# Three converted hi/lo weight buffers in place of two in a two-layer decoder trunk

## The chip, the cores and the metric

One NeuronCore of a Trainium2 chip runs the whole program. The metric is the device time of one execution in microseconds (us). The engines are PE (TensorE, with PEld for its weight loads), DVE (VectorE), ACT (ScalarE), POOL (GpSimd) and SP (SyncE, which here issues the plain DMAs). Each engine works through its own instructions in order and waits on semaphores of the others.

## The reference

272 tokens (16 meta tokens and 256) of width 1024 go through two layers. In each layer a recurrent group and an attention group mix the tokens; then a PEER stage picks, for each token and each of 8 heads, 16 of 16384 one-neuron experts:

```python
for l in range(DEPTH):
    z = rms_norm(h, mix_norm_g[l]) @ w_in[l]
    y_lru = rg_lru(...) * gelu(gate)
    y_att = mla_group(...)
    h = h + concat(rms_norm(y_lru), rms_norm(y_att)) @ w_out[l]
    h = h + peer(rms_norm(h, ffn_norm_g[l]), wq, subkeys, u, v)
# peer: s = (h @ wq) . subkeys; top 16 of the 16 x 16 sums; gates = softmax
uc = take(u, experts);  act = gelu(einsum('cd,ckd->ck', h, uc))
vc = take(v, experts);  out = einsum('ck,ckd->cd', gates * act, vc)
```

## The kernel before

All large weights come as blocks of 128 x 1024 fp32 (0.524 MB), in one list `order`: per layer 14 blocks of w_in, 8 of w_out, 16 of wq, 128 of uT and 128 of v. The mixing uses w_in and w_out; PEER uses the rest. For most tokens PEER is computed densely: all 16384 neurons (uT, then gelu, times a gate that is zero where an expert was not picked, then v). The gates are built for eight tokens at a time by one-hot tiles (`oha`, `ohb`: L950 to L957), PE products into a PSUM bank `ps_g` (L966), and a multiplication into `act` (`mult`, L976, with ACT's copy in L978 for the part not yet computed). For the last 32 tokens of layer 0 and 48 of layer 1 PEER is sparse: 16 experts of one head and token fill a partition each, and a gather (L1067, an indirect DMA issued by POOL) brings 128 rows of u or v into a tile. DVE consumes it: `dot` (L1050) multiplies rows of u with the tokens, `acc` (L1054) adds rows of v. There are 96 gathers of each layer, spread between the blocks of uT and v: some of u and v in uT, the others in v, one per about two blocks.

Both kinds of tile, blocks and gathers, take turns in one pool `raw` of PF = 7 buffers. `issue` starts the load of an entry of `order` as soon as the entry seven places ahead of it is converted. `conv` takes a block from `raw` and splits it into two fp16 halves: hi on ACT (L216), lo = block - hi on DVE (L217). They lie in a pool `hl`, so that PE can compute hi x (hi, lo) and lo x hi: 16 and 8 matmuls a block (`mm3`, L242 to L246, for wq and uT; `mv`, L1142, for v). A block's raw buffer is free when its lo is done, a gather's when its dot or acc is done. For v the activations themselves are split too: `ww`, by ACT L1129 and DVE L1130, for a pair of blocks at a time.

`block(kind, l, b)` returns the next pair of halves; before it does, it converts ahead:

```python
assert order[k] == (kind, l, b), (order[k], kind, l, b)
st["k"] = k + 1
conv(ahead(k, 1) + 1)
return hls.pop(k)
```

`ahead(k, n)` is the place of the n-th block after k. Converting a gather's entry means emitting its dot or acc there. The program is written in this order, but a scheduler in the language's runtime sets each engine's own order from a priority: hi and lo have a raised one (PRI = 40 places), all other work has its place in the source. Top-k, the gates and the onehot tiles (`pump`) run between the blocks on DVE and ACT.

`rows_of(g)` prepares a group of 16 sparse tokens: ACT copies L1017, PE transposes, ACT copies L1022.

Of the kernel before, what the change touches and what calls it, by code (L numbers as in the profile page):

```python
# [1 line left out]

# [1 line left out]

# [4 lines left out]
F32 = mybir.dt.float32  # L9
F32R = mybir.dt.float32r  # L10
F16 = mybir.dt.float16
# [10 lines left out]
S = 256  # L22
# [25 lines left out]
NU = (2, 2)  # L48
UB = (((64, 127, 16), (116, 124, 1)), ((60, 127, 32),))
PF = 7  # L50
ATT = ((3, 7), (1, 7))
LRU_AT = (1, 2, 3, 4)
LRU_FIRST = 0
# [88 lines left out]
def trunk(tc, a, out, dbg=None):  # L142
# [15 lines left out]
    with ExitStack() as ctx:  # L158
        per = ctx.enter_context(tc.tile_pool(name="per", bufs=1))
        raw_p = ctx.enter_context(tc.tile_pool(name="raw", bufs=PF))  # L160
        hl_p = ctx.enter_context(tc.tile_pool(name="hl", bufs=2))
        psp = ctx.enter_context(tc.tile_pool(name="psp", bufs=2, space=PSUM))
        PB = {"u": 2, "g": 2, "v": 4}

# [55 lines left out]
        def ahead(k, n):  # L220
            while n:
                k += 1
                if k < len(order) and order[k][0] != "gather":
                    n -= 1
                elif k >= len(order):
                    break
            return k

        def block(kind, l, b):
            k = st["k"]  # L230
            while order[k][0] == "gather":
                k += 1
            assert order[k] == (kind, l, b), (order[k], kind, l, b)
            st["k"] = k + 1
            conv(ahead(k, 1) + 1)
            return hls.pop(k)

        def mm3(o, w, xhi, xlo, first=True, n=8, off=0):
# [75 lines left out]
        def mixing(l, col, hh, hl, sq):  # L314
            SQ_H = [(one, sq[:, c]) for c in range(8)]
            C0 = NM if l else 0
            with tc.tile_pool(name="mix", bufs=1) as mp:
                def mt(shape, dt, name, bufs=1, tag=None):
                    return mp.tile(shape, dt, name=name, tag=tag or name, bufs=bufs)
# [323 lines left out]
                        yield from w_out_half(b, 0)  # L643

                late = []
                if l == 0:
                    s4 = [ps("v") for _ in range(4)]
                    for h in range(8):
                        w = s4[h % 4][:16, h // 4 * 16:h // 4 * 16 + 16]
                        P.matmul(w, qx[:, h, 0:16], kx[:, h, 0:16], start=True, stop=False, skip_group_check=True)  # L650
                        P.matmul(w, idb[:, 0:16], trib[:, 0:16], start=False, stop=True, skip_group_check=True)
                    mx = mt([16, 8], F32, "mx0")
                    sm = mt([16, 8], F32, "sm0")
                    p0 = mt([16, 8, 16], F32, "p0")
                    sv = mt([16, 8, 16], F32, "sv")
                    for h in range(4):
                        V.tensor_copy(sv.rearrange("p (a b) k -> p b a k", b=4)[:, h], s4[h][:16, :32].rearrange("p (a k) -> p a k", a=2))
                    V.tensor_reduce(out=mx, in_=sv, axis=AX.X, op=ALU.max)
                    V.tensor_tensor(out=p0, in0=sv, in1=bc(mx, 2, 16), op=ALU.subtract)
                    V.tensor_tensor(out=p0, in0=p0, in1=bc(rq[:16, 0, 2], 2, 16), op=ALU.mult)  # L660
                    A.activation(p0, p0, AF.Exp)
                    V.tensor_reduce(out=sm, in_=p0, axis=AX.X, op=ALU.add)
                    V.reciprocal(sm, sm)
                    tp = ps("g")
                    P.transpose(tp[:, 0:16], p0.rearrange("p a b -> p (a b)"), ident[:16, :16])
                    pt = mt([128, 256], F32, "pt", 2)
                    V.tensor_copy(pt[:, :16], tp[:, :16])
                    O = ps("u")
                    P.matmul(O[:16], pt[:, :16], v[:, 0], start=True, stop=True)
                    late.append(att_out(16, O, sm, 2, 0))  # L670

                fl = fills()
                for k, (q0, q1) in enumerate(QT):
# [22 lines left out]
                    def pv_t(h):  # L696
                        nt = k + 1
                        tp = ps("g")
                        for i in range(nt):
                            P.transpose(tp[:, i * 128:i * 128 + 128], Pm[:, h, 16 + i * 128:144 + i * 128], ident)  # L700
                        pt = mt([128, 256], F32, "pt", 2)
                        V.tensor_copy(pt[:, :nt * 128], tp[:, :nt * 128])
                        pts[h] = pt

# [20 lines left out]
                    pv_t(7)  # L725
                    pv_m(6)
                    pv_m(7)
                    pmc = mt([128, 8, 16], F32, "pmc", 2)
                    V.tensor_copy(pmc, Pm[:, :, 0:16])
                    tp = ps("g")  # L730
                    P.transpose(tp[:, 0:128], pmc.rearrange("p a b -> p (a b)"), ident)
                    pt = mt([128, 256], F32, "pt", 2)
                    V.tensor_copy(pt[:, :128], tp[:, :128])
                    P.matmul(O, pt[:, :128], v[:, 0], start=False, stop=True, skip_group_check=True)
                    V.reciprocal(sm, sm)
# [83 lines left out]
        def peer(l, col, hh, hl, rs, wq0):  # L819
            with tc.tile_pool(name="peer", bufs=1) as pp:  # L820
                SD = S - NSP[l]
                NF = NK * S - 256
                flata = pp.tile([128, NF], F32, name="act")
                act = flata[:, 0:NK * SD].rearrange("p (j t) -> p j t", t=SD)
                ready = set()
# [24 lines left out]
                ei = [egs[:, g, 0].bitcast(I32) for g in range(NG)]  # L850
                eg = [egs[:, g, 1] for g in range(NG)]
                dots = al([NG, 16], F32)
                cur[0], cur_end[0] = PS - 12800, PS
                rbs = al([T], F32)
                sk = al([2, 128], F32)
                dma(sk, a["sk"][l])
                rb = ps("g")
                rows(rs, rb, C0)
# [22 lines left out]
                i2T = pp.tile([128, S, 2], F16, name="i2T")  # L881
                gh = pp.tile([128, S, 2], F16, name="gh")
                gl = pp.tile([128, S], F32, name="gl")
                comb = pp.tile([128, 2, 128], F32, name="comb")

                bgq = []
                credit = [0.0]
# [118 lines left out]
                    yield 0.2  # L1006

                def sparse():
                    tail = [flata[:, NK * SD + i * D:NK * SD + i * D + D] for i in range(3)]
                    stage = tail[2]  # L1010
                    hrs = [tail[0], tail[1], None, None]
                    fin = []

                    def rows_of(g):
                        hr = hrs[g % 2 if g < NU[l] else 2 + g % 2]
                        for c in range(8):
                            A.activation(stage[:, c * 128:c * 128 + 128].rearrange("p (h t) -> p h t", h=8), bc(hns[:, c, g * 16:g * 16 + 16], 1, 8), AF.Copy)  # L1017
                        for c in range(0, 8, 4):
                            tp = ps("g")
                            for k in range(4):  # L1020
                                P.transpose(tp[:, k * 128:k * 128 + 128], stage[:, (c + k) * 128:(c + k) * 128 + 128], ident)
                            A.activation(hr[:, c * 128:c * 128 + 512], tp, AF.Copy)  # L1022
                        return hr

# [97 lines left out]
                    pump(PUMP[1] - prog["t"] / 960.0)  # L1122
                drain()
                pv = [ps("v") for _ in range(4)]
                ww = area("hn", F16, [128, 2, 2, 2, SD], "ww")

                def wsplit(j):
                    b = j // 2 % 2
                    A.activation(ww[:, b, 0], act[:, j:j + 2], AF.Copy)  # L1129
                    V.tensor_tensor(out=ww[:, b, 1], in0=act[:, j:j + 2], in1=ww[:, b, 0], op=ALU.subtract)  # L1130

                wsplit(0)
                for j in range(NK):
                    hi, lo = block("v", l, j)
                    if j % 2 and j + 1 < NK:
                        wsplit(j + 1)
                    wh, wl = ww[:, j // 2 % 2, 0, j % 2], ww[:, j // 2 % 2, 1, j % 2]

                    def mv(c, k):
                        o = pv[c // 2][:, (c % 2) * SD:(c % 2) * SD + SD]  # L1140
# [67 lines left out]
```

## Time and profile before

| | |
|---|---|
| median of 3 runs | 1668.75 us (1660.89 to 1672.01) |
| profiled execution | 1668.44 us, span 1666.7 us, mean clock 0.993 |
| PE / DVE / ACT / POOL busy | 1588.0 / 1503.8 / 1098.2 / 320.6 us |
| layer 0: mixing, wq and uT, v (by the first and last instructions of each) | about 0 to 140, to 538, to 846 |
| layer 1: the same | to 973, to 1364, to 1662 |

The time that an engine is busy is a mean over stages with different limits. In a row of waits the engine on the left stood still, and the instruction on the right is the one that came last; the numbers are the sum of us, how many times, and the longest one. In the view by stretch, the columns after the two times are busy us of PE, PEld, DVE, ACT and POOL, each with its number of instructions, then the granted clock of PE, the mean busy share of the DMA engines and the GB/s. PEld (loading weights) and PE (the matmuls) overlap, so their waits can be the same gap seen twice.

### The profile page before, as it was taken

Reading aid. Unit: us, or ns where it says so; the run is one execution under the profiler, and the core shown is the slowest. Engines: PE = TensorE matmul, PEld = TensorE weight load, DVE = VectorE, ACT = ScalarE, POOL = GpSimd, SP = SyncE. Lnnn points to the kernel's source line nnn. Section 1 sums busy time; section 2 is a strip of 40 time slices with the busy share of each in tenths; the row PEclk is TensorE's granted clock in tenths of the full one; section 3 lists DMA queues with packets and bytes.
Section 4 is the critical chain, followed back from the end, with each engine's and each line's share of the span. In section 5 each row is a group of like instructions: output and inputs, shape, how many; then the busy total and the mean of one; then the engine's idle time right before and its main releaser. Section 6 shows DMA issues by size and latency. Waiting matters only on the chain.

```text
span 1666.7 us, 40245 instructions
## 1 busy us (share of the span) xinstructions
PE 1588.0 (95%) x15926; PEld 1467.8 (88%) x15926; DVE 1503.8 (90%) x3074; ACT 1098.2 (66%) x2001; POOL 320.6 (19%) x256
## 2 busy tenths in 40 slices
PE   9989999999999999999999899899999999999997
PEld 6667798899999999999967687789988899999997
DVE  6889989889999999988978899997999998989886
ACT  6857565789987555555557565678988755555653
POOL 1000000101102333333210000002124124353253
PEclk9999999999999999999999999999999999999999
DMA  7305465667777999999973054567787899999995
GB/s 291 114 11 169 141 208 198 216 204 235 246 257 254 339 374 360 367 358 352 359 260 119 3 178 140 201 217 237 229 278 272 279 351 333 346 353 353 365 338 203
DMA packets 117709, 421.21 MB, mean 253 GB/s; under 512 B 14416, under 2 KB 15824, under 8 KB 117008
## 3 DMA queue, kind: packets, MB, share of 16 engines
q1 hardware_dynamic: 88592, 317.88, 54.2%
q0 software_dynamic: 28928, 100.76, 17.4%
q8 instruction: 124, 2.03, 0.5%
q14 instruction: 65, 0.53, 0.1%
HBM read 417.46 MB, written 1.05 MB: 251 GB/s over the span
## 4 chain that ended last, share of the span: by engine, by line
PE 40%; DVE 14%; DMA 5%; ACT 3%; issue 3%; POOL 1%; DVEq 0%; POOLq 0%; ACTq 0%
PE ps_v L1142 26%; DVE lo L217 6%; PE ps_u L246 3%; DMA raw<-v,act 3%; PE ps_u L242 3%; PE ps_u L243 3%; ACT hi L216 1%; PE ps_g L966 1%; DMA raw<-v 1%; POOL raw L1067 1%; DVE act L767 1%; DVE act L764 1%; PE ps_v L243 1%; PE ps_v L242 1%; PE ps_v L246 1%
## 5 line engine op out<-in xcount | busy, mean ns | idle before, releaser
L216 ACT ACTIVATE hi<-raw 128x1024 f16<-128x1024 f32 x588 | 619.8, 1055 | 430.8 <-PE ps_v L1142 208.6
L217 DVE SCALAR_TENSOR_TENSOR lo<-raw,hi 128x1024 f16<-128x1024 f32 x588 | 710.6, 1218 | 71.2 <-ACT hi L216 64.0
L1142 PE MATMUL ps_v<-ww,hi 128*128 128x224 f16 (+1 forms) x4096 | 426.8, 257 | 11.0 <-DVE ww L1130 10.1
L242 PE MATMUL ps_u<-hn,hi 128*128 128x224 f16 (+2 forms) x2112 | 413.1, 257 | 8.2 <-ACT hi L216 6.8
L243 PE MATMUL ps_u<-hn,hi 128*128 128x224 f16 (+2 forms) x2112 | 413.0, 256 | 0.0
L1142 PEld LDWEIGHTS <-hi 128*128 128x128 f16 x4096 | 382.5, 98 | 13.6 <-issue 12.5
L246 PEld LDWEIGHTS <-lo 128*128 128x128 f16 x2656 | 244.1, 98 | 54.0 <-DVE lo L217 43.2
L242 PEld LDWEIGHTS <-hi 128*128 128x128 f16 x2656 | 260.0, 98 | 27.5 <-ACT hi L216 11.5
L243 PEld LDWEIGHTS <-hi 128*128 128x128 f16 x2656 | 259.9, 98 | 14.8 <-issue 4.5
L246 PE MATMUL ps_u<-hn,lo 128*128 128x224 f16 (+2 forms) x2112 | 242.0, 257 | 25.4 <-DVE lo L217 24.7
L1142 PE MATMUL ps_v<-ww,lo 128*128 128x224 f16 (+1 forms) x2048 | 235.7, 257 | 5.4 <-DVE lo L217 5.0
L1067 POOL DMA_INDIRECT raw<-ur,act x96 | 131.2, 1367 | 467.6 <-DVE lo L217 237.4
L1067 POOL DMA_INDIRECT raw<-v,act x96 | 157.8, 1644 | 248.1 <-DVE lo L217 186.4
L1142 PEld LDWEIGHTS <-lo 128*128 128x128 f16 x2048 | 190.5, 98 | 10.8 <-DVE lo L217 10.0
L957 ACT ACTIVATE ohb<-oha,gl 128x128 f16<-128x128 f16 x432 | 138.7, 396 | 13.2 <-DVE oha L952 13.2
L1054 DVE SCALAR_TENSOR_TENSOR acc<-raw,act,acc 128x1024 f32<-128x1024 f32 x90 | 115.1, 1279 | 28.9 <-DMA raw<-v,act 28.8
L922 POOL DMA_DIRECT2D act<-comb x40 | 20.4, 518 | 599.0 <-DVE oha L952 310.6
L243 PE MATMUL ps_v<-hgx,hi 128*128 128x272 f16 (+1 forms) x480 | 113.6, 277 | 0.4 <-DVE hgx L311 0.4
L242 PE MATMUL ps_v<-hgx,hi 128*128 128x272 f16 (+1 forms) x480 | 113.3, 277 | 0.4 <-DVE hT L1183 0.3
L1050 DVE SCALAR_TENSOR_TENSOR raw<-raw,act 128x1024 f32<-128x1024 f32 x64 | 77.6, 1216 | 5.6 <-DMA raw<-ur,act 4.6
L1130 DVE TENSOR_TENSOR ww<-act,ww 128x448 f16<-128x448 f32 (+1 forms) x128 | 76.8, 600 | 0.0
L1129 ACT ACTIVATE ww<-act 128x448 f16<-128x448 f32 (+1 forms) x128 | 69.8, 547 | 0.0
(304 smaller groups left out, 1611.1 us busy)
## 6 DMA issues: line engine op xcount, KB each, us to landing
raw<-uT SPq DMA_DIRECT2D x256, 512.0 KB, 4.3
raw<-v SPq DMA_DIRECT2D x256, 512.0 KB, 6.2
raw<-wq SPq DMA_DIRECT2D x32, 512.0 KB, 3.3
raw<-w_in SPq DMA_DIRECT2D x28, 512.0 KB, 6.8
raw<-w_out SPq DMA_DIRECT2D x16, 512.0 KB, 3.3
uq<-uq SPq DMA_DIRECT2D x2, 1152.0 KB, 10.1
ukv<-ukv SPq DMA_DIRECT2D x2, 1024.0 KB, 8.2
raw<-ur,act POOLq DMA_INDIRECT x96, 6.5
```

The source lines that it names most:

```text
L216: A.activation(hi, r, AF.Copy, scale=WS)
L217: V.scalar_tensor_tensor(out=lo, in0=r, scalar=WS, in1=hi, op0=ALU.mult, op1=ALU.subtract)
L242: P.matmul(o, hi[:, s], xhi[:, c], start=first and c == 0, stop=False, skip_group_check=True)
L243: P.matmul(o, hi[:, s], xlo[:, c], start=False, stop=False, skip_group_check=True)
L246: P.matmul(o, lo[:, s], xhi[:, c], start=False, stop=c == n - 1, skip_group_check=True)
L957: A.activation(ob[:, 1, t], oe[:, t], AF.Copy, scale=gl[:, b * 8 + t:b * 8 + t + 1])
L1050: keep = V.scalar_tensor_tensor(out=t, in0=t, scalar=1.0, in1=hr, op0=ALU.mult, op1=ALU.mult, accum_out=dot[:, s:s + 1])
L1054: keep = V.scalar_tensor_tensor(out=acc, in0=t, scalar=dot[:, s:s + 1], in1=acc, op0=ALU.mult, op1=ALU.add)
L1067: G.indirect_dma_start(out=t, out_offset=None, in_=tab, in_offset=bass.IndirectOffsetOnAxis(ap=ei[g][:, s:s + 1], axis=0))
L1129: A.activation(ww[:, b, 0], act[:, j:j + 2], AF.Copy)
L1130: V.tensor_tensor(out=ww[:, b, 1], in0=act[:, j:j + 2], in1=ww[:, b, 0], op=ALU.subtract)
L1142: P.matmul(o, (hi, hi, lo)[k][:, s], (wh, wl, wh)[k], start=j == 0 and k == 0 and c % 2 == 0, stop=j == NK - 1 and k == 2, skip_group_chec ...
```

## The change

There are three hi/lo pairs instead of two (`NHL = 3`), and `block` converts two blocks ahead instead of one. The ww pairs go from two to four, and `wsplit` runs two pairs ahead. The space comes from three places: the staging area of `rows_of` is 512 columns wide instead of 1024, and is filled, transposed and copied twice; the mixing tiles `pt` and `pmc` are slices of one tile `pta` in the buffer of `sel0`, which is dead then; `comb` lies in the scratch part of the flat `act` tile. Line numbers rise by 2 to 5 (hi L216 to L218, lo L217 to L219, dot L1050 to L1054, acc L1054 to L1058, mult L976 to L980, ww L1130 to L1134). The number of instructions of each engine is the same.

```diff
 PF = 7
+NHL = 3
...
-        hl_p = ctx.enter_context(tc.tile_pool(name="hl", bufs=2))
+        hl_p = ctx.enter_context(tc.tile_pool(name="hl", bufs=NHL))
...
-            conv(ahead(k, 1) + 1)
+            conv(ahead(k, NHL - 1) + 1)
             return hls.pop(k)
...
+                pts_ = itertools.cycle((pta[:, 0:256], pta[:, 256:512]))
                 if l == 0:
...
+                    pt = next(pts_)
                     V.tensor_copy(pt[:, :16], tp[:, :16])
...
+                    pmc = pta[:, 512 + k * 128:640 + k * 128].rearrange("p (a b) -> p a b", a=8)
                     V.tensor_copy(pmc, Pm[:, :, 0:16])
...
+                NF = NK * S - 768
                 flata = pp.tile([128, NF], F32, name="act")
...
+                cur[0], cur_end[0] = PS - 13056, PS
                 rbs = al([T], F32)
                 sk = al([2, 128], F32)
+                comb = al([2, 128], F32)
                 dma(sk, a["sk"][l])
...
 
...
-                    stage = tail[2]
+                    tail = [flata[:, NK * SD + i * D:NK * SD + i * D + D] for i in range(2)]
+                    stage = flata[:, NK * SD + 2 * D:NK * SD + 2 * D + 512]
                     hrs = [tail[0], tail[1], None, None]
                     fin = []
 
                     def rows_of(g):
                         hr = hrs[g % 2 if g < NU[l] else 2 + g % 2]
-                        for c in range(8):
-                            A.activation(stage[:, c * 128:c * 128 + 128].rearrange("p (h t) -> p h t", h=8), bc(hns[:, c, g * 16:g * 16 + 16], 1, 8), AF.Copy)
                         for c in range(0, 8, 4):
                             tp = ps("g")
                             for k in range(4):
-                                P.transpose(tp[:, k * 128:k * 128 + 128], stage[:, (c + k) * 128:(c + k) * 128 + 128], ident)
+                                A.activation(stage[:, k * 128:k * 128 + 128].rearrange("p (h t) -> p h t", h=8), bc(hns[:, c + k, g * 16:g * 16 + 16], 1, 8), AF.Copy)
+                            for k in range(4):
+                                P.transpose(tp[:, k * 128:k * 128 + 128], stage[:, k * 128:k * 128 + 128], ident)
                             A.activation(hr[:, c * 128:c * 128 + 512], tp, AF.Copy)
                         return hr
...
-                ww = area("hn", F16, [128, 2, 2, 2, SD], "ww")
+                ww = area("hn", F16, [128, 4, 2, 2, SD], "ww")
 
                 def wsplit(j):
-                    b = j // 2 % 2
+                    b = j // 2 % 4
                     A.activation(ww[:, b, 0], act[:, j:j + 2], AF.Copy)
                     V.tensor_tensor(out=ww[:, b, 1], in0=act[:, j:j + 2], in1=ww[:, b, 0], op=ALU.subtract)
 
                 wsplit(0)
+                wsplit(2)
                 for j in range(NK):
                     hi, lo = block("v", l, j)
-                    if j % 2 and j + 1 < NK:
-                        wsplit(j + 1)
-                    wh, wl = ww[:, j // 2 % 2, 0, j % 2], ww[:, j // 2 % 2, 1, j % 2]
+                    if j % 2 and j + 3 < NK:
+                        wsplit(j + 3)
+                    wh, wl = ww[:, j // 2 % 4, 0, j % 2], ww[:, j // 2 % 4, 1, j % 2]
 
                     def mv(c, k):
                         o = pv[c // 2][:, (c % 2) * SD:(c % 2) * SD + SD]
```

What stands where in the order of the engines (x of the tile names are running numbers; `lo<-raw` converts a block, `acc2<-raw` and `raw,act<-raw,act` consume a gather, ww and act as above). First, DVE in v of layer 1, before: blocks 19839, 19904 and so on, gathers 19934, 19999. The tile numbers follow the order in which the tiles are loaded.

```order
L217 SCALAR_TENSOR_TENSOR lo_19972<-raw_19839,hi_19971 128x1024
L1054 SCALAR_TENSOR_TENSOR acc2_19603<-raw_19869,act_13729,acc2_19603 128x1024
L1130 TENSOR_TENSOR ww_19703<-act_13729,ww_19703 128x416
L217 SCALAR_TENSOR_TENSOR lo_20005<-raw_19872,hi_20004 128x1024
L217 SCALAR_TENSOR_TENSOR lo_20037<-raw_19904,hi_20036 128x1024
L1054 SCALAR_TENSOR_TENSOR acc2_19603<-raw_19934,act_13729,acc2_19603 128x1024
L1130 TENSOR_TENSOR ww_19703<-act_13729,ww_19703 128x416
L217 SCALAR_TENSOR_TENSOR lo_20070<-raw_19937,hi_20069 128x1024
L217 SCALAR_TENSOR_TENSOR lo_20102<-raw_19969,hi_20101 128x1024
L1054 SCALAR_TENSOR_TENSOR acc2_19603<-raw_19999,act_13729,acc2_19603 128x1024
```

After, DVE at the same place: blocks 19809, 19839, 19874, 19904, gathers 19936, 20001.

```order
L219 SCALAR_TENSOR_TENSOR lo_19942<-raw_19809,hi_19941 128x1024
L1134 TENSOR_TENSOR ww_19671<-act_13695,ww_19671 128x416
L1058 SCALAR_TENSOR_TENSOR acc2_19537<-raw_19936,act_13695,acc2_19537 128x1024
L219 SCALAR_TENSOR_TENSOR lo_19972<-raw_19839,hi_19971 128x1024
L219 SCALAR_TENSOR_TENSOR lo_20007<-raw_19874,hi_20006 128x1024
L1134 TENSOR_TENSOR ww_19671<-act_13695,ww_19671 128x416
L1058 SCALAR_TENSOR_TENSOR acc2_19537<-raw_20001,act_13695,acc2_19537 128x1024
L219 SCALAR_TENSOR_TENSOR lo_20037<-raw_19904,hi_20036 128x1024
L219 SCALAR_TENSOR_TENSOR lo_20072<-raw_19939,hi_20071 128x1024
```

Before, the gather of raw_19999 is issued when the lo of raw_19839 is done, and four lo's, two acc's and two ww's follow that lo ahead of its acc. After, the gather of raw_20001 is issued when the lo of raw_19809 is done; between it and its acc stand ww, acc, two lo's and ww. The acc moved ahead of the lo's of the blocks 19904 to 19969, which are loaded before it.

Second, DVE in v of layer 0: before,

```order
L217 SCALAR_TENSOR_TENSOR lo_8275<-raw_8169,hi_8274 128x1024
L1130 TENSOR_TENSOR ww_7870<-act_1814,ww_7870 128x448
L1050 SCALAR_TENSOR_TENSOR raw_8204,act_1814<-raw_8204,act_1814 128x1024
L217 SCALAR_TENSOR_TENSOR lo_8305<-raw_8172,hi_8304 128x1024
L217 SCALAR_TENSOR_TENSOR lo_8340<-raw_8234,hi_8339 128x1024
L1130 TENSOR_TENSOR ww_7870<-act_1814,ww_7870 128x448
L1050 SCALAR_TENSOR_TENSOR raw_8269,act_1814<-raw_8269,act_1814 128x1024
L217 SCALAR_TENSOR_TENSOR lo_8370<-raw_8237,hi_8369 128x1024
L217 SCALAR_TENSOR_TENSOR lo_8405<-raw_8272,hi_8404 128x1024
L1050 SCALAR_TENSOR_TENSOR raw_8302,act_1814<-raw_8302,act_1814 128x1024
```

and after, where the gather raw_8259 is issued when the lo of raw_8126, the first row, is done:

```order
L219 SCALAR_TENSOR_TENSOR lo_8230<-raw_8126,hi_8229 128x1024
L219 SCALAR_TENSOR_TENSOR lo_8262<-raw_8129,hi_8261 128x1024
L1054 SCALAR_TENSOR_TENSOR raw_8159,act_1800<-raw_8159,act_1800 128x1024
L1134 TENSOR_TENSOR ww_7858<-act_1800,ww_7858 128x448
L219 SCALAR_TENSOR_TENSOR lo_8295<-raw_8191,hi_8294 128x1024
L1054 SCALAR_TENSOR_TENSOR raw_8259,act_1800<-raw_8259,act_1800 128x1024
```

Before, the gather of raw_8302, issued when the lo of raw_8169 is done, has four lo's, two dots and two ww's ahead of its dot; after, the gather of raw_8259 has two lo's, a dot and a ww.

Third, DVE in uT of layer 1, at the products of the gates (`mult`, L976 and L980, two halves of 94 blocks). Before:

```order
L217 SCALAR_TENSOR_TENSOR lo_18387<-raw_18184,hi_18386 128x1024
L1120 TENSOR_TENSOR act_13729<-act_13729,gt2_14403 128x2x152
L954 TENSOR_TENSOR ohb_16085<-oha_16084,gh_13738 128x1024
L976 SCALAR_TENSOR_TENSOR act_13729<-act_13729,ps_g_18359 128x94x4
L976 SCALAR_TENSOR_TENSOR act_13729<-act_13729,ps_g_18368 128x94x4
L1050 SCALAR_TENSOR_TENSOR raw_18181,act_13729<-raw_18181,act_13729 128x1024
L217 SCALAR_TENSOR_TENSOR lo_18419<-raw_18216,hi_18418 128x1024
```

After:

```order
L219 SCALAR_TENSOR_TENSOR lo_18352<-raw_18149,hi_18351 128x1024
L1124 TENSOR_TENSOR act_13695<-act_13695,gt2_14368 128x2x152
L958 TENSOR_TENSOR ohb_16050<-oha_16049,gh_13704 128x1024
L980 SCALAR_TENSOR_TENSOR act_13695<-act_13695,ps_g_18327 128x94x4
L219 SCALAR_TENSOR_TENSOR lo_18387<-raw_18186,hi_18386 128x1024
L980 SCALAR_TENSOR_TENSOR act_13695<-act_13695,ps_g_18336 128x94x4
```

The block of raw_18184 before is that of raw_18149 after, and the next one, raw_18216, is raw_18186. Before, the lo of that next block stands behind both halves of `mult`; after, it stands between them. In uT each lo stands one block earlier against the other work on DVE.

## Rows read from the trace of the kernel before

**Rows 1.** The page, part 1: busy us, share of the span, instructions.

```profile
PE 1588.0 (95%) x15926; PEld 1467.8 (88%) x15926; DVE 1503.8 (90%) x3074; ACT 1098.2 (66%) x2001; POOL 320.6 (19%) x256
```

**Rows 2.** Busy time by stretch: PE, PEld, DVE, ACT, POOL; clock, DMA share, GB/s.

```profile
200.00:320.00 120.00, 109.51 (x1091) 102.01 (x1089) 114.69 (x368) 78.47 (x104) 2.54 (x5) 1.00 0.59 198
...
400.00:538.00 138.00, 137.22 (x1548) 136.34 (x1546) 134.91 (x197) 113.55 (x281) 20.81 (x15) 1.00 0.77 253
538.00:846.00 308.00, 303.30 (x3121) 299.74 (x3120) 278.77 (x325) 165.45 (x196) 97.40 (x85) 0.99 0.96 357
...
1020.00:1120.00 100.00, 86.76 (x900) 79.04 (x899) 99.92 (x346) 62.50 (x75) 0.00 (x0) 1.00 0.58 195
...
1200.00:1320.00 120.00, 110.64 (x1305) 105.83 (x1304) 119.99 (x183) 97.69 (x249) 31.73 (x20) 1.00 0.82 276
1320.00:1364.00 44.00, 41.74 (x463) 40.35 (x462) 41.53 (x56) 27.14 (x44) 12.40 (x10) 1.00 0.94 336
1364.00:1662.00 298.00, 285.77 (x3120) 280.61 (x3119) 257.70 (x283) 161.99 (x192) 120.52 (x61) 0.99 0.91 329
680.00:700.00 20.00, 20.00 (x211) 20.00 (x209) 18.57 (x19) 11.83 (x14) 6.47 (x6) 1.00 1.00 381
```

**Rows 3.** Waits in 195 to 538: us in total, times, longest.

```profile
ACT hi L216 <- PE ps_u L243: 41.0, 44, 1.8
...
PEld L246 <- DVE lo L217: 15.4, 26, 1.9
...
PEld L242 <- ACT hi L216: 3.7, 7, 1.1
```

**Rows 4.** Waits in 1027 to 1364.

```profile
PEld L246 <- DVE lo L217: 25.8, 40, 1.7
...
PEld L242 <- ACT hi L216: 7.5, 10, 1.6
ACT act L978 <- DVE act L976: 7.1, 8, 2.9
```

**Rows 5.** Waits in 1364 to 1662.

```profile
DVE acc L1054 <- DMA raw<-v,act: 21.5, 11, 4.1
...
PE ps_v L1142 <- DVE ww L1130: 9.6, 6, 2.6
```

**Rows 6.** Timeline of 1619 to 1629: start, duration, engine, line, operation.

```profile
1617.87 2.35 DVE L217 SCALAR_TENSOR_TENSOR lo<-raw,hi 128x1024 f16<-128x1024 f32 x2
...
1620.14 1.28 DVE L1054 SCALAR_TENSOR_TENSOR acc<-raw,act,acc 128x1024 f32<-128x1024 f32 x1
1620.49 4.52 POOL L1067 DMA_INDIRECT raw<-v,act  x1 [5.92 <-DVE lo L217]
...
1621.34 0.58 DVE L1130 TENSOR_TENSOR ww<-act,ww 128x416 f16<-128x416 f32 x1
...
1624.06 1.44 PEld L1142 LDWEIGHTS <-hi 128*128 128x128 f16 x16
...
1626.20 1.44 PEld L1142 LDWEIGHTS <-hi 128*128 128x128 f16 x16
```

**Rows 7.** Timeline of 1630 to 1636; in brackets the idle time before.

```profile
1632.21 1.28 DVE L1054 SCALAR_TENSOR_TENSOR acc<-raw,act,acc 128x1024 f32<-128x1024 f32 x1 [4.05 <-DMA raw<-v,act]
...
1634.05 0.88 PE L1142 MATMUL ps_v<-ww,hi 128*128 128x208 f16 x8 [2.60 <-DVE ww L1130]
```

**Rows 8.** The gathers of L1067, 340 to 538: from issue to landing.

```profile
DMA to landing us min/median/max: 4.2/5.0/7.8
```

**Rows 9.** The same, 538 to 846.

```profile
DMA to landing us min/median/max: 5.0/7.2/9.7
```

**Rows 10.** The same, 1164 to 1364.

```profile
DMA to landing us min/median/max: 4.0/5.3/9.7
```

**Rows 11.** The same, 1364 to 1662.

```profile
DMA to landing us min/median/max: 4.8/8.0/11.6
```

More of the change, by code (lines that the diff above doesn't have):

```diff
@@ L1 @@
 from contextlib import ExitStack
+import itertools
 import numpy as np
@@ L645, in mixing @@
                 late = []
+                pta = mt([128, 768], F32, "pta", tag="sel0")
+                pts_ = itertools.cycle((pta[:, 0:256], pta[:, 256:512]))
                 if l == 0:
@@ L665, in mixing @@
                     P.transpose(tp[:, 0:16], p0.rearrange("p a b -> p (a b)"), ident[:16, :16])
-                    pt = mt([128, 256], F32, "pt", 2)
+                    pt = next(pts_)
                     V.tensor_copy(pt[:, :16], tp[:, :16])
@@ L700, in pv_t @@
                             P.transpose(tp[:, i * 128:i * 128 + 128], Pm[:, h, 16 + i * 128:144 + i * 128], ident)
-                        pt = mt([128, 256], F32, "pt", 2)
+                        pt = next(pts_)
                         V.tensor_copy(pt[:, :nt * 128], tp[:, :nt * 128])
@@ L727, in mixing @@
                     pv_m(7)
-                    pmc = mt([128, 8, 16], F32, "pmc", 2)
+                    pmc = pta[:, 512 + k * 128:640 + k * 128].rearrange("p (a b) -> p a b", a=8)
                     V.tensor_copy(pmc, Pm[:, :, 0:16])
@@ L731, in mixing @@
                     P.transpose(tp[:, 0:128], pmc.rearrange("p a b -> p (a b)"), ident)
-                    pt = mt([128, 256], F32, "pt", 2)
+                    pt = next(pts_)
                     V.tensor_copy(pt[:, :128], tp[:, :128])
@@ L821, in peer @@
                 SD = S - NSP[l]
-                NF = NK * S - 256
+                NF = NK * S - 768
                 flata = pp.tile([128, NF], F32, name="act")
@@ L852, in peer @@
                 dots = al([NG, 16], F32)
-                cur[0], cur_end[0] = PS - 12800, PS
+                cur[0], cur_end[0] = PS - 13056, PS
                 rbs = al([T], F32)
                 sk = al([2, 128], F32)
+                comb = al([2, 128], F32)
                 dma(sk, a["sk"][l])
@@ L883, in peer @@
                 gl = pp.tile([128, S], F32, name="gl")
-                comb = pp.tile([128, 2, 128], F32, name="comb")
                 bgq = []
@@ L1008, in sparse @@
                 def sparse():
-                    tail = [flata[:, NK * SD + i * D:NK * SD + i * D + D] for i in range(3)]
-                    stage = tail[2]
+                    tail = [flata[:, NK * SD + i * D:NK * SD + i * D + D] for i in range(2)]
+                    stage = flata[:, NK * SD + 2 * D:NK * SD + 2 * D + 512]
                     hrs = [tail[0], tail[1], None, None]
```

## The prediction

> **What bounds the kernel now.** The profiled execution took 1668.44 us (span 1666.7), 0.3 us under the median of 1668.75, so I add up against the span and add that 0.3 at the end. I read the page's busy times first. TensorE is busy 1588.0 us, 95% [rows 1], but that is an average over stages, so the second view is the busy time by stretch [rows 2]: the last three columns there are the granted clock, the DMA share and GB/s. In 538 to 846 (v of layer 0) and 1364 to 1662 (v of layer 1) PE is busy 303.30 of 308 and 285.77 of 298 us: it idles 4.7 and 12.2 us. In 400 to 538, 1020 to 1120 and 1200 to 1320 VectorE (DVE) is busy 134.91 of 138, 99.92 of 100 and 119.99 of 120 us: there DVE sets the pace and PE has the gaps.
>
> The third view is the waits, by stretch. In wq and uT, PE's weight loads wait for lo 15.4 us (26 times) and for hi 3.7 us in layer 0 [rows 3], 25.8 and 7.5 us in layer 1 [rows 4]. In v of layer 1 the sequence is different [rows 5]: DVE's acc, which adds a gathered row, waits 21.5 us in 11 times for its gather's DMA, up to 4.1 us; ww stands behind acc on DVE; and PE waits 9.6 us for ww. One of these [rows 7]: acc starts at 1632.21 after 4.05 us on its DMA, and PE's matmuls at 1634.05 after 2.60 us on ww.
>
> **What the change does, part by part.** No instruction is added or removed that costs time; the order and the buffers change. A third hi/lo pair lets hi and lo run two blocks ahead of PE.
>
> (a) *wq and uT.* The stalls there sum to 52.4 us [rows 3, 4], but most lie where DVE never rests. A deeper buffer takes no work off DVE; it lets PE enter a busy stretch with one more block in hand, once. One block of v in layer 1 takes 1626.20 − 1624.06 = 2.14 us [rows 6], with 208 columns; layer 0 has 224, so 2.14 × 224 / 208 = 2.30 us. There are four such stretches, 200 to 320 and 400 to 538, 1020 to 1120 and 1200 to 1320: 2 × 2.30 + 2 × 2.14 = 8.9 us saved. In 1320 to 1364, PE idles 2.3 us with DVE at 41.53 of 44; I take half, 1.2. Against it stand the gathers of uT in layer 0: by the new order, four have only one lo and six or seven small operations between the lo that frees their buffer and their own consumer. DVE's mean instruction in 400 to 538 is 134.91 / 197 = 0.685 us [rows 2], so that is 1.2 + 6.5 × 0.685 = 5.6 us against a median landing of 5.0 and a longest of 7.8 [rows 8]: between 0 and 4 × 2.2 us; I take 1, near the median. Sum: −9.1 us, between −52 (all stalls gone) and 0.
>
> Here a rule of the Trainium skill (Perfetto Trace Analysis, Optimization Strategy) speaks the other way: gaps that repeat on the engine that should be saturated can mean that there are too few buffers. PE's repeating waits for lo would be such gaps, and by it up to 52.4 us would come back. The same page (Identifying the Most-Contended Engine) counts VectorE's occupancy as a fair measure of its limit, and DVE at 99.92 of 100 us agrees with that, so I keep 9.1.
>
> (b) *Staging.* `rows_of` now copies four blocks, transposes, copies the result, and repeats, so ScalarE (ACT) waits for PE inside it: two halves × six calls = 12 waits. The nearest row is hi's wait for PE, 41.0 us in 44 times, 0.93 each [rows 3]: 11 us if nothing hides it. ACT is busy 113.55 of 138 and 97.69 of 120 us there, and hi runs two blocks (4.6 us) ahead, which hides it. I take +1.
>
> (c) *v of layer 0.* PE idles 4.7 us, so −4.7 is the end below. The cost is that DVE's acc and dot come sooner after their buffer's release. Take T as the time from a gather's issue to its landing. DVE's durations [rows 6] are 1.17 for a lo (2.35 for two), 1.28 for acc (and for dot about the same) and 0.58 for ww; POOL issues 0.27 us after the releasing lo ends (1620.49 against 1617.87 + 2.35). Before, the least that stood between the release and the consumer was three lo's, two accs and two ww's: 3.5 + 2.6 + 1.2 − 0.3 = 7.0 us against a median T of 7.2 [rows 9]. After, by the order, seven gathers have about two lo's, one dot, one ww (3.9 us; the second excerpt of the order shows one), ten have two more accs or dots in place of one (5.2 us) and eight have 6.5. At T = 7.2 DVE would wait 7 × 3.3 + 10 × 2.0 + 8 × 0.7 = 49 us. DVE idles 308 − 278.77 = 29.2 us there, which swallows the first part: +20 is the upper end. At T = 6 it is 23 us, less than the idle time, but not in the right places. I take +4.
>
> A second rule would limit the gain here: the Trainium skill (DMA: Bandwidth & Descriptors, Where 436 GB/s comes from) puts about 358 GB/s as HBM's limit for one core. By it v of layer 0, at 357 GB/s over the whole stretch, could gain nothing. The trace moved 381 GB/s in 680 to 700 [rows 2], so the measurement leaves a few per cent.
>
> (d) *v of layer 1* decides. Here the order shows a steady pattern of two lo's, ww, acc per two blocks. Before, a gather's buffer was released by a lo after which two accs, two ww's and four lo's stood ahead of its own acc: 2.6 + 1.2 + 4.7 − 0.3 = 8.2 us at DVE's pace, about the median landing of 8.0 [rows 11]. After, 50 of the 64 gathers have only two lo's, two ww's and one acc (or dot) between (the first excerpt). Let A(n) be the start of the n-th acc. The releasing lo ends one acc and two lo's after A(n−1): 1.28 + 2.35 = 3.63 us; + 0.27 for POOL, + T, and A(n+1) can start. So two periods take at least 3.9 + T, and one period P = (3.9 + T) / 2. PE wants 2 × 2.14 = 4.28 us per period, so the pattern hides T only to 4.7 us. The least landing is 4.0 in uT, 5.0 and 4.8 in v, and v's medians are 7.2 and 8.0 [rows 8 to 11]. An extra hi/lo pair pays for one late acc, but not for fifty in a row, since DVE runs in order and every lo stands behind an acc.
>
> T itself falls when the DMA queues are emptier: its medians are 5.0 us where the stretch nearest to it moves 253 GB/s, 5.3 at 276, 8.0 at 329, 7.2 at 357 [rows 2, 8 to 11]. A period moves three tiles of 0.524 MB. On the line from 276 to 357, T = 6.2 gives P = 5.05, thus 311 GB/s, at which the line reads 6.1: consistent. On the line from 276 to 329 the consistent point is 6.55. I take 6.2, an estimate. Cost: 50 × (5.05 − 4.28) = 38.5 us. What goes away is the present idle time, 12.2 us, and the 1% of clock lost in 298 us (0.99 [rows 2]), 3.0: net +23. The same sum for T = 4.8, 5.3, 7.2 and 8.0 gives −12, +1, +48 and +68.
>
> (e) *The rest* costs nothing: `comb` in the scratch space, the smaller staging area and the shared mixing tiles change addresses, and no row shows an engine waiting on them; the ww pairs two ahead remove PE's wait for ww, which is in (d).
>
> **Sum.** −9.1 + 1 + 4 + 23 = +18.9: 1668.44 + 18.9 = 1687.3, and with the 0.3 to the median, 1688 us.
>
> **The rivals.** *A: it gains.* If a gather that is alone at the head of emptier queues lands within 4.8 us, everything else holds: −9.1 − 4.7 − 12 = −26, 1643 us. For it: the least landings, 4.0 in uT and 4.8 in v, and that the times fall with the load. Against: [rows 9, 11], where no median in v is under 7. It decides at T = 4.7. *B: no change.* T = 5.3, as at 276 GB/s [rows 10]: −9.1 + 1 + 4 + 1 = −3, 1666 us. Against: 311 GB/s is nearer to 329. *C: much slower.* If T does not fall with the load and stays at the medians 7.2 to 8.0, v of layer 1 costs 48 to 68 and v of layer 0 about 12: 1721 to 1741 us. The point is whether T is queueing or the gather's own time. *D: the gate products.* `mult` stands a lo later on DVE (third excerpt), with PE's matmuls where they were; the two gate banks come free one lo (1.17 us) later. Nearest row: ACT's gate copies wait 7.1 us in 8 times for `mult` [rows 4]. If about half of the 27 products of each layer hold PE for 0.6 us, 54 × 0.5 × 0.6 = 16 us come on top and (a) turns into a loss: 1704 us. By the order, the change does do what it says: each lo of uT stands one block earlier against the work around it.
>
> **How the numbers follow.** Chances: my forecast (T from 5.6 to 6.8, 1675 to 1702 us) 0.36, A 0.22, B 0.22, C 0.14, D 0.06. A measurement of this kernel can tell about 1% from no change. Faster by over 1% (under 1652) is most of A: 0.20. Within 1% (to 1685.4) is B, the edge of A and a third of the forecast: 0.36. Slower is the rest of the forecast, C and D: 0.44. The range leaves a tenth at either side: half of A below 1638 to 1643, and the upper half of C above 1735. I take 1638 to 1735; the forecast's own range is 1675 to 1702.
>
> **What would show it.** In the changed kernel, v of layer 1 (298 us now, 1364 to 1662) should last about 320; acc's wait for its DMA there should go from 21.5 us in 11 times to some 35 us in 40 or more, short and regular; the gathers' median landing should fall from 8.0 to about 6, and the rate from 329 to about 310 GB/s. PE's waits for lo in wq and uT should shrink by about 9 us, not vanish, with DVE still at 99% in 1020 to 1120 and 1200 to 1320. I am wrong if acc rarely waits (T under 4.7, A), or if the uT stages lose their stalls altogether, which would mean that the gaps came from the two buffers and not from DVE's work.

## The result, and the profile after

The changed kernel is slower: 1758.5 us in the median, against 1668.85 (now four runs of each), a ratio of 1.0547 (95% interval 1.0496 to 1.0598). I forecast 1688 and a range up to 1735: the sign was right and the size was not. The profiled execution spans 1757.1 us, 90.4 more than before.

The page, part 1, of the changed kernel, against [rows 1]:

```profile
PE 1614.5 (92%) x15926; PEld 1487.8 (85%) x15926; DVE 1502.5 (86%) x3074; ACT 1095.3 (62%) x2001; POOL 303.5 (17%) x256
```

DVE's, ACT's and POOL's work is the same within 6%, and no engine got more to do; but PE is busy 26.5 us longer for the same matmuls, and it waits for the rest of the 90.4. Where they lie, I read from the first and the last matmul of each stage in the trace (all in us; uT is counted up to the first matmul of v):

| run | wq ends | uT, layer 0 | v, layer 0 | to the end of wq, layer 1 | uT, layer 1 | v, layer 1 |
|---|---|---|---|---|---|---|
| before | 195.2 | 343.2 | 307.4 | 181.5 | 336.7 | 297.6 |
| changed | 195.6 | 347.5 | 346.2 | 181.1 | 339.3 | 342.4 |
| difference | +0.4 | +4.3 | +38.8 | −0.4 | +2.6 | +44.8 |

The differences sum to 90.5. Both v stages lose, and uT, where the gain was to come, loses 7. A stage is read from one execution: v of layer 0 takes 307.4 us here and 311.1 in the kernel before with four gate banks, whose v is the same (the last run below), so differences of about 4 us in a v stage say nothing. Busy time by stretch, for v of the two layers (columns as in [rows 2]):

```profile
543.00:890.00 347.00, 315.43 (x3126) 305.23 (x3126) 279.57 (x343) 166.23 (x202) 135.46 (x84) 0.97 0.88 316
```

```profile
1409.00:1753.00 344.00, 300.11 (x3124) 288.46 (x3123) 256.50 (x282) 162.25 (x197) 71.61 (x61) 0.96 0.82 285
```

In v of layer 0 PE's idle time grew from 308 − 303.30 = 4.7 us to 31.6, its busy time from 303.30 to 315.43; in v of layer 1 from 12.2 to 43.9, and from 285.77 to 300.11. The DMA rate fell from 357 and 329 GB/s to 316 and 285: the DMA engines are not the limit. The waits of v in layer 0, then in layer 1:

```profile
DVE acc L1058 <- DMA raw<-v,act: 34.8, 23, 2.7
PEld L1147 <- DVE lo L219: 31.6, 22, 4.2
DVE raw L1054 <- DMA raw<-ur,act: 26.8, 8, 5.1
```

```profile
DVE acc L1058 <- DMA raw<-v,act: 54.8, 24, 3.8
PEld L1147 <- DVE lo L219: 49.1, 31, 3.9
...
DVE raw L1054 <- DMA raw<-ur,act: 19.4, 12, 6.0
```

The consumers of the gathers wait for their DMA 61.6 us in layer 0 and 74.2 us in layer 1. Before, these waits were 13.2 us in layer 0,

```profile
DVE acc L1054 <- DMA raw<-v,act: 7.3, 11, 1.8
...
DVE raw L1050 <- DMA raw<-ur,act: 5.9, 7, 1.6
```

and acc waited 21.5 us in 11 times in layer 1 [rows 5]. PE then waits for lo, since every lo stands behind such a consumer on DVE. The gathers of v in layer 0 and in layer 1, from issue to landing (7.2 and 8.0 in [rows 9, 11]):

```profile
DMA to landing us min/median/max: 5.3/7.8/11.1
```

```profile
DMA to landing us min/median/max: 4.4/6.4/8.9
```

So the median rose in layer 0 and fell in layer 1, while the rate fell in both: the rate alone doesn't set the landing. The timeline of three periods in v of layer 1:

```profile
1465.19 1.28 DVE L1058 SCALAR_TENSOR_TENSOR acc<-raw,act,acc 128x1024 f32<-128x1024 f32 x1 [3.24 <-DMA raw<-v,act]
...
1467.67 0.89 PE L1147 MATMUL ps_v<-ww,lo 128*128 128x208 f16 x8 [2.53 <-DVE lo L219]
...
1468.39 1.59 PE L1147 MATMUL ps_v<-ww,hi 128*128 128x208 f16 x16
...
1469.02 1.05 POOL L1071 DMA_INDIRECT raw<-v,act  x1 [6.25 <-DVE lo L219]
1469.16 1.28 DVE L1058 SCALAR_TENSOR_TENSOR acc<-raw,act,acc 128x1024 f32<-128x1024 f32 x1
...
1470.36 2.35 DVE L219 SCALAR_TENSOR_TENSOR lo<-raw,hi 128x1024 f16<-128x1024 f32 x2
...
1470.53 1.59 PE L1147 MATMUL ps_v<-ww,hi 128*128 128x208 f16 x16
...
1476.20 1.28 DVE L1058 SCALAR_TENSOR_TENSOR acc<-raw,act,acc 128x1024 f32<-128x1024 f32 x1 [2.99 <-DMA raw<-v,act]
1477.40 2.35 DVE L219 SCALAR_TENSOR_TENSOR lo<-raw,hi 128x1024 f16<-128x1024 f32 x2
...
1478.68 0.89 PE L1147 MATMUL ps_v<-ww,lo 128*128 128x208 f16 x8 [2.28 <-DVE lo L219]
...
1479.40 2.48 PE L1147 MATMUL ps_v<-ww,hi 128*128 128x208 f16 x16
...
1480.18 1.28 DVE L1058 SCALAR_TENSOR_TENSOR acc<-raw,act,acc 128x1024 f32<-128x1024 f32 x1
```

Here is the mechanism, with a feature that I had not seen. The acc at 1476.20 consumes the gather issued at 1469.02, 7.2 us earlier. The next one, at 1480.18, finds its gather landed. The gathers form two chains, odd and even; here they don't share the delay as equal short waits, but every second acc waits for both: 7.04 and 3.98 us between starts, 5.51 in the mean, and 2.99 us of waiting at once. (So it is in most of 1442 to 1567; among the dots from 1598 to 1651 no wait is over 1.7 us.) PE stands still for 2.28 us, and some of the matmuls after that are slower: sixteen take 2.48 us at 1479.40, where they took 1.59 at 1470.53. Not every long wait is followed by that: after 2.53 us at 1467.67 sixteen took 1.59. What decides it I leave open. The granted clock of the whole stretch is 0.96, a mean over its two levels of 2.4 and 1.2 GHz (0.99 in [rows 2]).

### The profile page after: what moved, and what is told of

Read it like the earlier page. It is cut to its first block, busy times and chain, and to the rows that moved or that the text cites. A ratio compares the mean times of both kernels' runs of the same rounds, so it can differ in the third digit from the quotient of the medians.

```text
span 1757.1 us, 40278 instructions
## 1 busy us (share of the span) xinstructions
PE 1614.5 (92%) x15926; PEld 1487.8 (85%) x15926; DVE 1502.5 (86%) x3074; ACT 1095.3 (62%) x2001; POOL 303.5 (17%) x256
## 5 line engine op out<-in xcount | busy, mean ns | idle before, releaser
L218 ACT ACTIVATE hi<-raw 128x1024 f16<-128x1024 f32 x588 | 618.6, 1055 | 484.6 <-PE ps_v L1147 176.7
L219 DVE SCALAR_TENSOR_TENSOR lo<-raw,hi 128x1024 f16<-128x1024 f32 x588 | 707.8, 1218 | 44.8 <-ACT hi L218 34.6
L1147 PE MATMUL ps_v<-ww,hi 128*128 128x224 f16 (+1 forms) x4096 | 438.5, 262 | 5.3 <-ACT ww L1133 4.2
L1147 PEld LDWEIGHTS <-hi 128*128 128x128 f16 x4096 | 391.4, 100 | 10.8 <-issue 5.9
L1147 PE MATMUL ps_v<-ww,lo 128*128 128x224 f16 (+1 forms) x2048 | 242.0, 262 | 67.8 <-DVE lo L219 67.6
L244 PEld LDWEIGHTS <-hi 128*128 128x128 f16 x2656 | 260.7, 98 | 19.4 <-issue 6.3
L245 PEld LDWEIGHTS <-hi 128*128 128x128 f16 x2656 | 260.8, 98 | 19.0 <-issue 8.0
L248 PEld LDWEIGHTS <-lo 128*128 128x128 f16 x2656 | 248.3, 98 | 31.8 <-DVE lo L219 20.9
L1147 PEld LDWEIGHTS <-lo 128*128 128x128 f16 x2048 | 191.6, 100 | 83.5 <-DVE lo L219 80.7
L248 PE MATMUL ps_u<-hn,lo 128*128 128x224 f16 (+2 forms) x2112 | 243.2, 258 | 13.4 <-DVE lo L219 13.2
L1071 POOL DMA_INDIRECT raw<-ur,act x96 | 125.4, 1306 | 504.8 <-DVE lo L219 332.6
L1071 POOL DMA_INDIRECT raw<-v,act x96 | 146.7, 1528 | 305.9 <-DVE lo L219 245.2
L1058 DVE SCALAR_TENSOR_TENSOR acc<-raw,act,acc 128x1024 f32<-128x1024 f32 x90 | 115.4, 1282 | 90.1 <-DMA raw<-v,act 89.6
L926 POOL DMA_DIRECT2D act<-act x40 | 20.3, 518 | 603.8 <-DMA raw<-uT 308.6
L1054 DVE SCALAR_TENSOR_TENSOR raw<-raw,act 128x1024 f32<-128x1024 f32 x64 | 77.9, 1217 | 19.2 <-DMA raw<-ur,act 15.7
L1134 DVE TENSOR_TENSOR ww<-act,ww 128x448 f16<-128x448 f32 (+1 forms) x128 | 76.9, 602 | 0.0
L970 PE MATMUL ps_g<-ohb,oha 128*128 128x128 f16 x864 | 59.7, 220 | 14.3 <-ACT act L982 14.3
```

Of the source, the lines that this page charges most:

```text
L218: A.activation(hi, r, AF.Copy, scale=WS)
L219: V.scalar_tensor_tensor(out=lo, in0=r, scalar=WS, in1=hi, op0=ALU.mult, op1=ALU.subtract)
L244: P.matmul(o, hi[:, s], xhi[:, c], start=first and c == 0, stop=False, skip_group_check=True)
L245: P.matmul(o, hi[:, s], xlo[:, c], start=False, stop=False, skip_group_check=True)
L248: P.matmul(o, lo[:, s], xhi[:, c], start=False, stop=c == n - 1, skip_group_check=True)
L970: P.matmul(g[:, t * 128:t * 128 + 128], oa[:, s * 4 + t], ob[:, k, s * 4 + t], start=t == 0 and k == 0, stop=t == 3 and k == 1, skip_group ...
```

## The experiments

The theory: in v, what counts is the DVE work that stands between the lo that releases a gather's buffer and the gather's own consumer (the distance). If it is shorter than the landing, DVE waits. The change shortened the distance, by the place where the consumers and the ww splits now stand. The rivals: the third hi/lo pair or the added ww buffers cost by themselves (their reads and writes), or the space edits do. The distances below are sums of the durations in [rows 6] over each kernel's order; DVE's busy time between release and consumer in the traces gives the same within 0.5 us (for v of layer 1, in the median, 4.8 us in the changed kernel, 7.2 with three pairs alone, 9.8 with the consumers held).

**The space edits alone.** The changed kernel with two hi/lo pairs and the old `wsplit`.

```diff
-NHL = 3
+NHL = 2
...
-                ww = area("hn", F16, [128, 4, 2, 2, SD], "ww")
+                ww = area("hn", F16, [128, 2, 2, 2, SD], "ww")
...
-                    b = j // 2 % 4
+                    b = j // 2 % 2
...
-                wsplit(2)
...
-                    if j % 2 and j + 3 < NK:
-                        wsplit(j + 3)
+                    if j % 2 and j + 1 < NK:
+                        wsplit(j + 1)
-                    wh, wl = ww[:, j // 2 % 4, 0, j % 2], ww[:, j // 2 % 4, 1, j % 2]
+                    wh, wl = ww[:, j // 2 % 2, 0, j % 2], ww[:, j // 2 % 2, 1, j % 2]
```

> The space edits alone (half-width staging, shared mixing tile, comb in scratch), two hi/lo pairs and two ww pairs as before. Theory (gathers' consumers moved too close to their buffers' release): the order on DVE in v is that of before, so both v stages last as before (307 and 298 us) and the total is 1668 plus at most 5 for the staging. Rival (the staging or the scratch space costs): 1680 or more, with the excess in uT.

Ratio 1.0017 (0.9984 to 1.005), stages 343.2, 306.7, 336.7 and 299.2. The space costs nothing that can be measured, between −3 and +8 us; term (b), +1, lies within that.

**Each half of the change alone.** The four ww pairs with two hi/lo pairs (only the first edit above), and the three hi/lo pairs with the old `wsplit` (only the rest of it).

> The space edits and four ww pairs split two pairs ahead, but two hi/lo pairs. By its order on DVE, 21 gathers of v in layer 0 have under 6 us of work between release and consumer (17 in the changed kernel, 0 before), but none in v of layer 1 (8.2 us in the median, as before). Theory: v of layer 0 grows from 307 to about 345 us, v of layer 1 stays at 298 within 5, total 1700 to 1715. Rival (the third hi/lo pair itself costs, by its reads and writes beside PE): no stage grows, 1669.

> The space edits and three hi/lo pairs two blocks ahead, but two ww pairs as before. By its order, no gather of v in layer 0 has under 6 us (6.9 at least, as before); in v of layer 1 52 of 64 have 6.9 us (8.2 before, 4.6 in the changed kernel). Theory: v of layer 0 307 within 8; v of layer 1 with landings of 7 to 8 us grows by 0 to 25, so 298 to 323; total 1670 to 1695. Rival (the third pair itself): both v stages as in the changed kernel, 346 and 342, total near 1755.

| run | ratio | v, layer 0 | v, layer 1 |
|---|---|---|---|
| four ww pairs alone | 1.0281 (1.0223 to 1.0339) | 351.2 | 302.3 |
| three hi/lo pairs alone | 1.0188 (1.0107 to 1.0268) | 311.7 | 316.1 |
| both (the change) | 1.0547 (1.0496 to 1.0598) | 346.2 | 342.4 |

The stages part as their distances do. (The two totals, 1719.96 and 1698.8 us, lie a little above those expected.) The ww lead alone, with two hi/lo pairs, loses 43.8 us in v of layer 0, all that the change loses there, and 4.7 in v of layer 1, which has as many ww splits; so it is not their reads and writes that cost. The third pair alone spares v of layer 0 (+4.3, within the spread) and loses 18.5 us in layer 1, where its distance is 6.9 us. Why the scheduler places the consumers of layer 0 earlier when ww is split earlier, no run shows. It takes both together to reach 4.6 us of distance and 342 us. That a third pair costs by itself is refuted in layer 0 by the second of these runs, and by the next ones. The waits of v in layer 0 with four ww pairs alone, then in layers 0 and 1 with three hi/lo pairs alone:

```profile
PEld L1147 <- DVE lo L219: 41.1, 21, 4.5
...
DVE raw L1054 <- DMA raw<-ur,act: 27.7, 10, 6.8
DVE acc L1058 <- DMA raw<-v,act: 23.5, 14, 5.2
```

```profile
DVE acc L1058 <- DMA raw<-v,act: 17.2, 17, 2.7
...
DVE raw L1054 <- DMA raw<-ur,act: 4.6, 5, 2.8
```

```profile
DVE acc L1058 <- DMA raw<-v,act: 39.8, 29, 2.9
PEld L1146 <- DVE lo L219: 24.8, 23, 2.2
```

**The consumers held back.** The whole change, but a gather's consumer is written where it stood before, one block ahead of PE, while blocks are converted two ahead. The loads that take buffers after a held gather's are issued later to match.

```diff
+        held = []
+
+        def step(n):
+            while held and held[0][0] < n:
+                g, r = held.pop(0)
+                hook["step"](r, *order[g][2])
+
         def conv(n):
...
-                issue(k + PF)
+                issue((held[0][0] if held else k) + PF)
...
                 if order[k][0] == "gather":
-                    hook["step"](r, *order[k][2])
+                    held.append((k, r))
                     continue
...
+            step(ahead(k, 1) + 1)
             conv(ahead(k, NHL - 1) + 1)
```

> The whole change, but the consumer of a gather is written one block later (at the distance of before), while blocks are converted two ahead. By its order, v of layer 1 has 9.4 us between release and consumer (8.2 before, 4.6 after), v of layer 0 has 9 gathers under 6 us (17 after). Theory: v of layer 1 falls from 342 to 298 or less, v of layer 0 to 315 to 330, total 1670 to 1695. Rival (the third pair or the ww lead itself): both v stages stay over 335, total over 1740.

Then the same with two ww pairs (the ww lines of the first edit above):

> Three hi/lo pairs two blocks ahead, gathers' consumers one block later as in the held version, and two ww pairs as before. By its order every gather of v has 8.7 us or more of DVE work between release and consumer. Theory (the stages follow that distance alone): v of layer 0 falls from the 323 us of the held version to 300 to 308, v of layer 1 stays at 288 to 296, total 1650 to 1664, at or a little under the kernel before. Rival (three pairs cost in v by something else): v of layer 0 stays over 315, total 1675 or more.

| run | ratio | v, layer 0 | v, layer 1 |
|---|---|---|---|
| consumers held, four ww pairs | 1.0041 (1.0004 to 1.0078) | 322.6 | 292.7 |
| consumers held, two ww pairs | 0.9921 (0.9889 to 0.9952) | 304.3 | 287.3 |

Both came out as the theory has it: 50 us of v of layer 1 come back with the third pair still there, and the rest of layer 0 with the old ww. The last version beats both kernels, by 0.8% the one before, at 1657.77 us in the median. Its v stages in the view by stretch (layer 0, then layer 1) show what a third pair is worth when nothing is moved too close:

```profile
538.00:843.00 305.00, 301.37 (x3124) 299.85 (x3123) 277.23 (x323) 165.15 (x199) 117.32 (x84) 1.00 0.98 360
```

```profile
1366.00:1654.00 288.00, 284.08 (x3124) 281.87 (x3123) 257.23 (x282) 160.63 (x196) 82.72 (x61) 0.99 0.92 338
```

PE idles 3.6 and 3.9 us there, where it idled 4.7 and 12.2. In its waits, acc no longer shows among those that hold DVE; ACT's hi waits for its block's load instead:

```profile
ACT hi L225 <- DMA raw<-v: 79.4, 69, 2.9
```

**Held back two blocks.** The distance longer once more: `step(k + 1)` in place of `step(ahead(k, 1) + 1)`.

> As the held version with two ww pairs, but the gathers' consumers are written two blocks later than in the changed kernel, so a gather of v has 9.9 us or more of DVE work between release and consumer (8.7 and 9.3 in the held version with two ww pairs). If the distance is already longer than nearly every landing there, both v stages stay within 3 us of 304 and 287, total 1650 to 1662. If landings over 9 us still held DVE, v of layer 1 falls below 284. If the blocks behind the later-freed gather buffers come too late now, ACT's hi waits for its DMA grow and v of layer 0 goes over 310.

Ratio 1.0074 (1.0044 to 1.0104); v of layer 0 320.5 us, of layer 1 288.8. The third outcome came: a gather that keeps its raw buffer for another block delays the loads that take buffers after it. hi's wait for its load in v of layer 0 goes from 79.4 to

```profile
ACT hi L225 <- DMA raw<-v: 100.4, 70, 3.5
```

So the best of the distances tried has an edge on either side, the far one in v of layer 0. That the seven raw buffers set both edges is my reading; no run changes their number.

**What the landing is made of.** The changed kernel with a plain load in place of each gather; the rows of the experts that were picked are left out.

```diff
-                    G.indirect_dma_start(out=t, out_offset=None, in_=tab, in_offset=bass.IndirectOffsetOnAxis(ap=ei[g][:, s:s + 1], axis=0))
+                    G.dma_start(out=t, in_=tab[(g * 16 + s) * 128:(g * 16 + s) * 128 + 128])
```

> The changed kernel, with each gather replaced by a plain load of 128 consecutive rows of the same table on the same queue: same bytes, same place in every order; the rows of the experts that were picked are left out. If the 6.4 and 7.8 us from issue to landing are queueing in the DMA engines, the landing stays within 0.7 us and both v stages over 335 us. If they are the gather's own (index reading, one descriptor for a row), the landing falls to 5 or less, like that of the blocks or below, and the v stages to 300 to 320.

One execution: 1691.5 us, v stages 316.6 and 306.1 us. From issue to landing, in layer 0 and in layer 1:

```profile
DMA to landing us min/median/max: 3.6/6.7/8.3
```

```profile
DMA to landing us min/median/max: 4.1/5.5/7.4
```

Neither of the two answers was right: the landing is 1.1 and 0.9 us shorter, not 0.7 nor under 5. About 1 us is the gather's own (in this kernel, against a plain load on the same queue), the rest stays. The landing is counted from the start of POOL's instruction, and that instruction is itself shorter for a plain load, in layer 1 by 0.5 of the 0.9 us (median 1055 ns, then 527):

```profile
L1071 POOL DMA_INDIRECT raw<-v,act x45: 950/1055/2190, 1408.9 to 1728.4; - x45
```

```profile
L1071 POOL DMA_DIRECT2D raw<-v x42: 527/527/530, 1392.7 to 1665.3; - x42
```

But the stages answer strongly: 0.9 to 1.1 us of landing are worth 30 and 36 us of stage, far over the spread of a stage. This shows that the landing sets the pace of v in the changed kernel, with the order untouched. Of the landing that remains, how much is queueing isn't settled.

**uT.** The gate products in the four banks that uT leaves unused, in the held version with two ww pairs, and in the kernel before:

```diff
                         for s in range(2):
-                            g = ps("g")
+                            g = ps("v")
```

> As the held version with two ww pairs, with the gate products in the four banks that uT leaves unused instead of the two g banks. Theory (in uT the later multiplication holds the gate banks, so that PE waits for them): PE's waits for the copies out of the gate bank (about 10 us in layer 1 of the changed kernel) vanish and uT of layer 1 falls by 4 to 8 us against the same version with two banks; total 1642 to 1656. Rival (DVE's work sets uT, the waits only change their name): uT stages within 2 us of the version with two banks.

> The kernel before with the gate products in the four banks that uT leaves unused. Theory (in the kernel before the two banks did not hold PE, 0.7 us in the waits): no change, 1669 within 5. Rival (four banks help by themselves): uT of both layers shorter by 4 us or more, under 1662.

The rival was right in the first: uT of layer 1 took 342.2 us with four banks and 343.0 with two, and the totals are 0.9942 (0.9914 to 0.9969) and 0.9921 of before. The waits did change their name. With two banks, in wq's end and uT of layer 1:

```profile
PEld L256 <- DVE lo L226: 12.2, 17, 1.9
PEld L978 <- issue: 12.1, 12, 2.8
...
PE ps_g L978 <- ACT act L990: 10.3, 11, 2.6
```

With four, the last row is gone, and PE waits for lo again:

```profile
PEld L256 <- DVE lo L226: 17.7, 24, 2.0
```

The kernel before with four banks is at 1.0005 (0.9974 to 1.0037), as expected.

## Why the prediction failed

**The mechanism and the place** of (d) held: the consumers of gathers came too close to the release, DVE waits, PE waits for lo. (b) and the space edits of (e) held by the first run. The ww pairs of (e) did not: they were put at nothing beside PE's wait for ww, and alone they cost 43.8 us in v of layer 0, because they too move the consumers. Three terms of the sum were mis-sized, and one of them is a step that was wrong.

**(c), v of layer 0: +4 forecast, +38.8 measured.** This is the step that failed. I worked out 49 us of DVE waiting at T = 7.2 and let DVE's 29.2 us of idle time swallow most of it. The waits for gathers came to 61.6 us (T was 7.8), 48 more than the 13 that were there before, and DVE's idle time went from 29.2 to 347 − 279.57 = 67.4 us, 38 more: it swallowed 10 of the 48, not most of them. PE had 4.7 us to give. Taken as +49 − 4.7, the term would have been about 44. The order from which (c) counted was that of the whole change, so the 49 us hold the part of the ww lead without naming it; by the runs of each half, that part is all of it.

**(d), v of layer 1: +23 forecast, +44.8 measured.** The chain of the sum was right, the T put into it was too small. The median T was 6.4 us, against my 6.2, and gives (3.9 + 6.4) / 2 = 5.15 us per period, 50 × 0.87 = 43.5, and less 12.2 and 3.0 only +28. But the gather that lands later sets the pace of both chains, and the early landing of the other gives nothing back. In the timeline the later one took 7.2 us from issue to acc, the period was 5.51, and the prediction's own line for T = 7.2 says +48. (As an estimate, since those periods are not the whole stage: the prediction's three tiles of 0.524 MB per period at the stage's 285 GB/s give 5.5 us too.) I also counted 3.0 us of clock as won, and the waits as short and regular. In this stage PE's busy time grew by 14.3 us instead, and in v of layer 0 by 12.1. By the granted clock about 11 and 7 us of that are clock (344 × 0.04 − 298 × 0.01 and 347 × 0.03 − 308 × 0.01, an estimate from rounded values); half speed follows some of the long waits. I don't add this to the price of the waits: in the timeline DVE goes on from the acc at 1480.18 without a wait while PE's slow matmuls run, so they fill time in which PE would have stood still.

**(a), wq and uT: −9.1 forecast, +7 measured.** That a deeper buffer gives little where DVE sets the pace held: in layer 1 uT's matmuls took 335.3 us from first to last before, and 335.5 in the changed kernel. The rule weighed against it (the Trainium skill, Perfetto Trace Analysis, Optimization Strategy: repeating gaps can mean too few buffers) would have given up to 52 us back; no run of uT agrees with it. PE's waits for lo did shrink, from 25.8 us in [rows 4], but they came back as waits around the gate products, rival D; in the changed kernel, in the same stages:

```profile
PEld L248 <- DVE lo L219: 12.2, 17, 1.9
...
PE ps_g L970 <- ACT act L982: 9.6, 12, 2.1
```

More banks, in the held version, sent them back to lo. The one block of credit for each stretch, 8.9 us in all, appears in no run.

The +4.3 us of layer 0 are the gathers of uT, which (a) took at 1 us, and at 2.2 each at most. No dot waited for its gather there before. With the change three did, 7.4 us in all, and with the consumers held and two ww pairs 0.9 us are left and the stage takes 342.6 us:

```profile
DVE raw L1054 <- DMA raw<-ur,act: 7.4, 3, 5.8
```

```profile
DVE raw L1062 <- DMA raw<-ur,act: 0.9, 1, 0.9
```

The +2.6 us of layer 1 lie almost whole between uT's last matmul and v's first, 1.3 us apart before and 3.8 after. There the first ww of v stands on ACT behind the hi of a later block, which waits for its load:

```profile
1407.79 1.06 ACT L218 ACTIVATE hi<-raw 128x1024 f16<-128x1024 f32 x1 [1.49 <-DMA raw<-v]
...
1409.15 1.85 ACT L1133 ACTIVATE ww<-act 128x416 f16<-128x416 f32 x4
1409.74 0.87 PE L1147 MATMUL ps_v<-ww,hi 128*128 128x208 f16 x8 [3.37 <-ACT ww L1133]
```

With the consumers held, uT's own matmuls of layer 1 take 337.0 to 341.4 us; why, I leave open.

**The chances.** C was the nearest of the cases (1721 to 1741). Its condition, that T stays at 7.2 to 8.0, held in layer 0 (7.8), and in layer 1 for the gather that is waited for (7.2), while the median there fell to 6.4. What C lacked is layer 0, which it had at about 12 us. A and B had nearly half the chance; both rested on T near 5, and the medians were 7.8 and 6.4.

## What to carry to other kernels

A deeper buffer, and an earlier split just as much, changes the places of everything that is written relative to it. Look at each transfer whose buffer is released and whose consumer stands in the same in-order engine, and count the work between the two. In this kernel the stages lost where that work was shorter than the landing under load, and of two neighbouring transfers the later one counted, not the median. When a deeper buffer loses, hold the consumers of the other streams at their old places before giving it up: here the same third pair, with two ww pairs again, gave 0.9921 in place of 1.0547. And don't pay a wait in an engine's chain from that engine's idle time: here 48 us more of waiting became 38 us more of idle time.

## What the runs showed that I had not expected

The waits of a chain through two alternating buffers can gather in every second member (7.04 and 3.98 us between starts). PE's busy time grew by 12.1 and 14.3 us for the same matmuls, and the clock of the stretches fell to 0.97 and 0.96. And v of layer 0 of the best version moved 360 GB/s over 305 us at a DMA share of 0.98.
